# A two-layer encoder on one core: v, q's sums and the attention output turned in 32x32 blocks on VectorE instead of on TensorE

## The chip, the cores and the metric

The kernel runs on one core of one Trainium2 chip. The metric is device time in microseconds of one execution; runs of the kernel before gave 774.77, 776.28 and 776.96, with the median 776.28. Profiles come from one further execution, in which the hardware profiler recorded every instruction. Engines in the profile: PE is TensorE's matrix multiply, PEld its loading of weights, DVE is VectorE, ACT ScalarE, POOL GpSimd, and SP the engine that only issues DMAs here.

## What is computed

Two pre-norm residual layers over 256 tokens of 1024 channels, in float32, and a final RMSNorm. Each layer projects the normalised input once into eleven segments, and runs two token mixers beside each other, a gated delta rule in both directions and a differential softmax attention:

```python
h = rmsnorm(x, norm_w[l]); proj = h @ w_in[l]
# delta branch: 8 heads of 128, chunks; q, k, v pass a 5-tap convolution and SiLU
qkv = silu(short_conv(concatenate([q, k, v]), conv_w))
q, k = l2norm(heads(q)), l2norm(heads(k))            # per token and head
o = rmsnorm(o_fwd + o_bwd, norm_w)                    # delta rule forward and backward
y_a = o * silu(z_a)
# attention branch: 8 heads, two softmaxes of 64 channels each
a = softmax(q0 k0) - lam * softmax(q1 k1)
y_b = rmsnorm(a @ v, subln_w) * (1 - lambda_init) * silu(z_b)
x = x + (sigmoid(gate_a) * (y_a @ w_pa) + sigmoid(gate_b) * (y_b @ w_pb)) @ w_out
```

## The kernel before

**Projections.** Tokens lie in two tiles of 128 (`NM` is 2). Every float32 product is made of three matmuls in the rounded format fp32r: each weight tile and each activation is split into a rounded part `hi` and the rest `lo`, and hi·hi, lo·hi and hi·lo are summed in PSUM (lines 244 to 246, 282, and 298 to 302). `weights` (L207) loads a pair of 128-row weight tiles over SP's queue into `raw`, which ScalarE rounds into `hi` (L230) and VectorE subtracts to `lo` (L232). Three raw, two hi and two lo buffers let this run two pairs ahead of TensorE. A projection of 512 columns is 48 matmuls. In `proj_tm` (L237) and `proj_by_tile` (L259) tokens are the output rows; in `proj_fm` (L287) channels are.

**Turning.** A 128x128 transpose is a matmul against `ident` into PSUM. `split_T` (L184) turns four of them and writes hi and lo from there. It serves h, the two gated outputs yb and ya, and the merged output. In `conv` (L517), channels are rows while the taps run along tokens (L524, L528) and SiLU follows (L532, L537); then each pair of channel tiles is turned (L545). For k the turned tile is copied (L552) and its squares summed per token by ScalarE (L557); for q only the squares are summed, into `ssq`; for v the turned tile is scaled by `nrm`, k's factor, on VectorE (L548).

**The delta chain.** k's sums and the gates give log decays (`log_decays`, L567). `decays` (L618) loads them broadcast from DRAM, 512 KB for four heads and one token tile, over POOL's queue (L622), masks them with affine_select (L628) and has ScalarE take the exponentials, 32 per layer (L632). `weigh_k` and `weigh_q` multiply products k·k and k·q by them (L639, L643). `turn_blocks` (L654) moves 32x32 diagonal blocks through DRAM, `substitute` (L670) inverts them on VectorE in 31 steps, `spread_blocks` (L677) writes the result to DRAM (`udr`), and `merges` (L701) reads it back (L709, L713) and joins blocks to 64 and 128. `chunks` (L779) then runs the states: y1, sp, ks, y2, qs, po, each four matmuls per group of four heads, copied out of PSUM by ScalarE or VectorE before the next. Its output lands in q's place in `kq` (L818, L828).

**Attention.** `head` (L834) makes two score products on two row halves of TensorE (L844), maxima on VectorE (L851), exponentials on ScalarE (L853), the difference on VectorE (L861), four turns (L864), the product with v (L870) and its sum of squares (L876).

**Order.** A scheduler orders each engine's instructions by priority, which follows the program's order unless `tc.high_priority` raises it, and by when its own time model has them ready. `behind(ins)` queues an instruction behind `ins` where both are on the same engine; it adds no wait. `mark` keeps the instructions that these refer to; `mark["done", kt]` is the last matmul of step kt of the latest `proj_tm`. Per layer the program has: v of attention, k (two convolutions), log decays, q (two), decays and k·k, q and k of attention, substitution, v (two), then heads 0 to 7 among the projections zb and za, merges and chunks at high priority, the gating of yb (`gated`, L955), the projections gb, pb, ga, the gating of ya, pa, the merged output and o. The long projections fill TensorE while the chains wait for other engines.

**Rings.** `work` and `wpool` hand out buffers by tag: `w2c` has three of 2 KB per partition, shared by small tiles of several stages; `vf` two.

The functions that the diff touches, and what calls them, with the profile's line numbers:

## Time and profile before

| | |
|---|---|
| median of three runs | 776.28 us (774.77 to 776.96) |
| the profiled execution | 779.15 us |
| its span, first to last instruction | 777.3 us |
| mean granted TensorE clock | 0.995 |
| PEld busy | 649.4 us, 84% |
| a turn of 128x128 on TensorE, record | 270 to 273 ns |
| HBM | 121.27 MB read, 4.75 MB written |

A busy share is the share of the span in which an engine ran at least one instruction. Records of matmuls overlap, because they are pipelined: what one costs is the distance from its start to the next start, and not its duration. In a group's line, the numbers behind the shapes are the count, the busy time in us, the mean ns of one, and the idle time of the engine ahead of them with what ended it. In a waits line they are the total, the times and the longest. The chain of waits follows the execution back from its last instruction, from each step to what released it. Layer 0 takes about the first half of the span and layer 1 the second; the two look alike.

### The profile page before, as it was taken

To read this page: it belongs to the slowest core of one execution; us is meant where nothing else is said; L and a number is where in the kernel's file an instruction comes from. 1 tells how busy PE (TensorE), PEld (TensorE's weight loads), DVE (VectorE), ACT (ScalarE), POOL (GpSimd) and SP (SyncE) were. 2 spreads that over 40 slices of the span, in tenths; PEclk is the share of its full clock that TensorE was granted. 3 is DMA by queue.
4 is the path that set the end of the run, shared out by engine and by line. 5 is a ranking of instruction groups with operands and counts; after the bars stand their busy time and mean duration, and the time that the engine had idled before them with its cause. 6 is when DMAs were issued, how large, how long until landed. Compare 5 with 4: busy or idle time off the path is not lost.

```text
span 777.3 us, 13803 instructions
## 1 busy us (share of the span) xinstructions
PE 758.6 (98%) x5222; PEld 649.4 (84%) x5222; DVE 562.4 (72%) x1057; ACT 470.8 (61%) x1036; POOL 98.8 (13%) x137
## 2 busy tenths in 40 slices
PE   7999999999999999999999998999999999999996
PEld 4899889977878888877889888989788788888784
DVE  5686889999974635377677777999998653536782
ACT  5647776556767744564455668565677676356551
POOL 5100422100320000010010034210005010001000
PEclk9999999999999999999999999999999999999998
DMA  7762767654594544346675255766557754343631
GB/s 226 220 195 61 216 191 205 179 172 126 153 204 147 193 135 136 109 156 206 207 224 140 78 165 217 200 181 175 142 147 179 186 163 161 114 133 112 213 110 54
DMA packets 77745, 126.91 MB, mean 163 GB/s; under 512 B 19679, under 2 KB 20015, under 8 KB 77680
## 3 DMA queue, kind: packets, MB, share of 16 engines
q1 hardware_dynamic: 71038, 112.99, 49.5%
q0 software_dynamic: 3936, 9.77, 4.6%
q10 hardware_dynamic: 2706, 3.28, 1.3%
q8 instruction: 41, 0.67, 0.4%
q14 instruction: 24, 0.20, 0.1%
HBM read 121.27 MB, written 4.75 MB: 162 GB/s over the span
## 4 chain that ended last, share of the span: by engine, by line
PE 79%; DVE 10%; DMA 5%; ACT 3%; issue 2%; POOL 0%; SPq 0%; POOLq 0%; DVEq 0%; ACTq 0%
PE pp_vb L282 5%; PE pp_qk L244 2%; PE sc L844 2%; PE pp_qk L245 2%; PE pp_o L282 2%; DMA raw_vb<-in_w_in_dram 2%; PE pp_qk L246 2%; PE av L870 2%; PE pp_za L245 2%; PE pp_gb L245 2%; PE pp_gb L244 2%; PE pp_za L246 2%; PE pp_pb L246 2%; PE pp_pb L245 2%; PE pp_ga L246 2%
## 5 line engine op out<-in xcount | busy, mean ns | idle before, releaser
L245 PE MATMUL pp_qk<-lo_qk,hT 128*128 128x512 f32 x128 | 50.6, 395 | 0.0
L246 PE MATMUL pp_qk<-hi_qk,hT 128*128 128x512 f32 x128 | 50.0, 390 | 0.0
L244 PE MATMUL pp_qk<-hi_qk,hT 128*128 128x512 f32 x128 | 45.5, 396 | 0.0
L232 DVE TENSOR_TENSOR lo_pb<-raw_pb,hi_pb 128x1024 fp32r<-128x1024 f32 x16 | 19.6, 1224 | 35.7 <-ACT hi_pb L230 35.7
L230 ACT CAST hi_qk<-raw_qk 128x1024 fp32r<-128x1024 f32 x28 | 29.4, 1051 | 26.1 <-PE pp_qk L246 15.5
L232 DVE TENSOR_TENSOR lo_qk<-raw_qk,hi_qk 128x1024 fp32r<-128x1024 f32 x32 | 39.1, 1221 | 6.0 <-ACT hi_qk L230 5.7
L298 PE MATMUL pf_q<-hT,hi_q 128*128 128x256 f32 x128 | 37.0, 292 | 1.8 <-DVE hi_q L230 1.8
L853 ACT ACTIVATE es<-sc,mx 128x256 f32<-128x256 f32 x64 | 29.8, 474 | 13.0 <-DVE mx L851 13.0
L302 PE MATMUL pf_q<-hT,lo_q 128*128 128x256 f32 x128 | 36.6, 299 | 0.7 <-DVE lo_q L232 0.6
L300 PE MATMUL pf_q<-hT,hi_q 128*128 128x256 f32 x128 | 36.5, 288 | 0.0
L298 PE MATMUL pf_v<-hT,hi_v 128*128 128x256 f32 x128 | 36.2, 287 | 0.0
L300 PE MATMUL pf_v<-hT,hi_v 128*128 128x256 f32 x128 | 35.9, 284 | 0.0
L298 PE MATMUL pf_k<-hT,hi_k 128*128 128x256 f32 x128 | 35.8, 285 | 0.0
L300 PE MATMUL pf_k<-hT,hi_k 128*128 128x256 f32 x128 | 35.6, 283 | 0.0
L232 DVE TENSOR_TENSOR lo_gb<-raw_gb,hi_gb 128x1024 fp32r<-128x1024 f32 x16 | 19.6, 1224 | 21.5 <-ACT hi_gb L230 21.3
L232 DVE TENSOR_TENSOR lo_ga<-raw_ga,hi_ga 128x1024 fp32r<-128x1024 f32 x16 | 19.6, 1225 | 21.0 <-ACT hi_ga L230 21.0
L302 PE MATMUL pf_k<-hT,lo_k 128*128 128x256 f32 x128 | 34.4, 284 | 0.4 <-DVE lo_k L232 0.4
L302 PE MATMUL pf_v<-hT,lo_v 128*128 128x256 f32 x128 | 34.5, 288 | 0.0
L230 ACT CAST hi_pb<-raw_pb 128x1024 fp32r<-128x1024 f32 x16 | 16.8, 1049 | 25.1 <-PE pp_pb L246 24.3
L528 DVE SCALAR_TENSOR_TENSOR cvq<-pf_q,cw,cvq 128x254 f32<-128x254 f32 (+1 forms) x64 | 29.5, 476 | 1.9 <-ACT cvq L524 1.4
L528 DVE SCALAR_TENSOR_TENSOR cvk<-pf_k,cw,cvk 128x254 f32<-128x254 f32 (+1 forms) x64 | 28.5, 478 | 2.0 <-ACT cvk L524 1.3
L528 DVE SCALAR_TENSOR_TENSOR cvv<-pf_v,cw,cvv 128x254 f32<-128x254 f32 (+1 forms) x64 | 29.8, 479 | 0.0
(358 smaller groups left out, 2496.9 us busy)
## 6 DMA issues: line engine op xcount, KB each, us to landing
raw_qk<-in_w_in_dram SPq DMA_DIRECT2D x32, 512.0 KB, 3.8
raw_k<-in_w_in_dram SPq DMA_DIRECT2D x16, 512.0 KB, 4.8
raw_q<-in_w_in_dram SPq DMA_DIRECT2D x16, 512.0 KB, 3.7
raw_v<-in_w_in_dram SPq DMA_DIRECT2D x16, 512.0 KB, 3.7
raw_zb<-in_w_in_dram SPq DMA_DIRECT2D x16, 512.0 KB, 3.7
raw_za<-in_w_in_dram SPq DMA_DIRECT2D x16, 512.0 KB, 4.5
raw_gb<-in_w_in_dram SPq DMA_DIRECT2D x16, 512.0 KB, 4.7
raw_o<-in_w_out_dram SPq DMA_DIRECT2D x16, 512.0 KB, 4.6
```

Source lines behind the costliest of these rows:

```text
L230: high = (V.tensor_copy if kp in turned else S.copy)(hi[:, :, :n], raw[:, :, :n]).ins
L232: mark[nm, kp] = high, V.tensor_tensor(lo[:, :, :n], raw[:, :, :n], hi[:, :, :n].bitcast(F32), ALU.subtract).ins
L244: T.matmul(o, act[kt // 4][:, 0, kt % 4, ts_], hi, start=kt == 0, stop=False)
L245: T.matmul(o, act[kt // 4][:, 0, kt % 4, ts_], lo, start=False, stop=False)
L246: mark["proj"] = T.matmul(o, act[kt // 4][:, 1, kt % 4, ts_], hi, start=False, stop=kt == KT - 1).ins
L282: mark["proj"] = T.matmul(o, a_, w_, start=kt == 0 and a_ is ah and w_ is hi, stop=kt == KT - 1 and a_ is al).ins
L298: T.matmul(o, hi[:, cs], act[kt // 4][:, 0, kt % 4, :], start=first, stop=False, skip_group_check=True)
L300: T.matmul(o, hi[:, cs], act[kt // 4][:, 1, kt % 4, :], start=False, stop=False, skip_group_check=True)
L302: T.matmul(o, lo[:, cs], act[kt // 4][:, 0, kt % 4, :], start=False, stop=done, skip_group_check=True)
L528: V.scalar_tensor_tensor(ca[:, o0:o1], acc[:, b, o0 + sft : o1 + sft], cw[:, j, cb : cb + 1], ca[:, o0:o1], ALU.mult, ALU.add)
L844: mm = T.matmul(sp[n][:, qt * SEQ : (qt + 1) * SEQ], qkT[h // 4][rows, 0, h % 4, qt * P : (qt + 1) * P], qkT[h // 4][rows, 1, h % 4, :], s ...
L853: S.activation(es[:, n, qt, :], spv[:, qt, :], AF.Exp, bias=mx[:, n, qt : qt + 1], accum_out=s_all[:, h, n, qt : qt + 1])
```

## The change

Three sets of turns leave TensorE. A block transpose on VectorE turns the sixteen 32x32 blocks of each 128x128 square in place, for four squares (512 columns) at once; a write of 256 KB to DRAM and four reads of 64 KB, all issued by POOL, then put the blocks where a full transpose would have them. This serves v (both tiles of a pair in one transpose, k's factor applied by ScalarE as it copies the landed blocks into `vtm`) and yb (`split_B` in place of `split_T`). For q's sums, `key_sums` transposes blocks, squares them on ScalarE, sums 32 at a time on VectorE, and passes only the partial sums through DRAM.

Beside that: the loads of the decays of heads 4 to 7 are queued behind POOL's last affine_select of heads 0 to 3's first tile (`cut`), where `seen` held ScalarE's exponentials; heads 1 to 5 get fixed places behind the middle or the end of a projection, with their four scores kept together; `weigh_q` and the first merge products move to the projection za 1; and pa's third weight pair gets a home in A's memory.

```diff
+    def squares(nm):
+        return work.tile([P, 4, 4, 32], F32, tag="tb", name=f"tb_{nm}", bufs=2)
+    def turn_squares(tb, src):
+        return V.transpose(tb, src.rearrange("p k (j t) -> p j k t", j=4)).ins
+    def bounce(tb, nm):
+        dd = dram.tile([4, 32, 4, P], F32, tag="bnc", name=f"bnc_{nm}", bufs=4)
+        G.dma_start(out=dd.rearrange("i t j x -> (i t) (j x)"), in_=tb.rearrange("p j k t -> p (j k t)"))
+        land = work.tile([P, 4, 4, 32], F32, tag="w2c", name=f"land_{nm}", bufs=3)
+        for j in range(4):
+            G.dma_start(out=land[blk(j)].rearrange("t i k d -> t i (k d)"),
+                        in_=dd[:, :, j].rearrange("i t x -> t i x"))
+        return land
+    def split_B(dst, src, m, nm, w):
+        tb = squares(f"{nm}{m}")
+        turn_squares(tb, src)
+        land = bounce(tb, f"{nm}{m}")
+        flat_ = squares(f"w{nm}{m}").rearrange("p a b t -> p a (b t)")
+        S.activation(flat_.rearrange("p k (i t) -> p k i t", i=4), land.rearrange("p i k t -> p k i t"),
+                     AF.Copy, scale=w)
...
+        S.copy(hi, flat_)
+        V.tensor_tensor(lo, flat_, hi.bitcast(F32), ALU.subtract)
...
+                if seg == "q":
+                    return
+                if seg == "v":
+                    tb = squares(f"v{l}{g}{b0}")
+                    turn_squares(tb, ths.rearrange("p b (m t) -> p (b m) t", m=NM))
+                    land = bounce(tb, f"v{l}{g}{b0}")
+                    for b in range(2):
+                        for m in range(NM):
+                            hd = 4 * g + b0 + b
+                            S.activation(vtm[:, m, hd, :].rearrange("p (i d) -> p i d", i=4),
+                                         land[:, :, 2 * b + m, :], AF.Copy, scale=nrm[:, m, hd : hd + 1])
+                    return
...
-                if seg == "v":
-                    V.tensor_tensor(vtm[:, :, bs, :].rearrange("p m b d -> p b m d"), ptv,
-                                    last(nrm[:, :, bs].rearrange("p m b -> p b m"), P), ALU.mult)
-                    return
...
+                mark["cut"] = G.affine_select(
...
-            first = mark["done", 5] if g == 0 else None
+            first = mark["done", 7] if g == 0 else None
...
+        def key_sums():
+            for h in range(0, NH, 2):
+                tb = squares(f"q{l}{h}")
+                with behind(mark["spread"]):
+                    turn_squares(tb, kq[:, h : h + 2, :, 1, :].rearrange("p h m t -> p (h m) t"))
+                S.activation(tb, tb, AF.Square)
+                V.tensor_reduce(qpart[:, :, h : h + 2, :].rearrange("p j h m -> p j (h m)"), tb,
+                                AX.X, ALU.add)
+            G.dma_start(out=qdr.rearrange("i t j x -> (i t) (j x)"),
+                        in_=qpart.rearrange("p j h m -> p (j h m)"))
+            for j in range(4):
+                G.dma_start(out=qsum[blk(j)], in_=qdr[:, :, j].rearrange("i t x -> t i x"))
+            V.tensor_reduce(ssq.rearrange("p m h -> p h m"),
+                            qsum.rearrange("p i (h m) -> p h m i", m=NM), AX.X, ALU.add)
...
-                for n in (1, 0):
+                for n in (1, 0) if after is None else (0, 1):
...
-                    with nullcontext() if n else tc.high_priority(offset=HP):
+                    with behind(None if qt or n or after is None else mark["done", after]), \
+                            tc.high_priority(offset=HP) if qt or not n or after is not None else nullcontext():
...
-        seen = mark["decay", 0], mark["decay", 1]
+        cut = mark["cut"]
...
-        decays(1, 0, seen[0])
+        decays(1, 0, cut)
...
-        decays(1, 1, seen[1])
+        decays(1, 1, cut)
...
-        head(1)
+        head(1, 7)
...
-        head(2)
-        head(3)
+        head(2, 3)
+        head(3, 7)
...
-        head(4)
-        head(5)
+        head(4, 3)
+        head(5, 7)
+        z_part(za, C_ZA, "za", 1)
         for g in range(2):
             for c in range(NM):
-                weigh_q(g, c, mark["done", 4 * g + 2 * c + 1])
-        z_part(za, C_ZA, "za", 1)
+                weigh_q(g, c, mark["done", 2 * g + c])
+        key_sums()
...
+        gated(lambda i, m: heads4(ob[i][:, m, :]), zb, rb, nw[:, 1:2], ybT, f"yb{l}",
+              split=split_B)
...
-        branch(yaT, w_pa[l], gta, f"pa{l}")
+        branch(yaT, w_pa[l], gta, f"pa{l}", [None, None, *homes((("A", 1),), f"pa{l}"), None])
...
-                later={2: mark[f"pa{l}0", 1], 3: mark[f"pa{l}0", 3]})
+                later={2: mark[f"pa{l}0", 2], 3: mark[f"pa{l}0", 3]})
```

More of the change, by code (lines that the diff above doesn't have):

```diff
@@ L833, in hybrid_encoder, with head @@
         ob = e4(f"ob{l}", "eo")
-        def head(h):
+        def head(h, after=None):
             es = work.tile([P, 2, NM, SEQ], F32, tag="w4a", name=f"es{l}{h}", bufs=2)
@@ L846, in head @@
                                       qkT[h // 4][rows, 1, h % 4, :], start=True, stop=True)
-                    if qt or not n:
+                    if qt or n != (after is None):
                         tc.keep_in_program_order(mm)
```

36 lines of the change are left out of this document (20 added, 16 removed).

## The prediction

> **What bounds the kernel now.** I read the page's engine line first, then the table by windows for three stretches that the change touches, then the waits of TensorE.
>
> ```profile
> PE 758.6 (98%) x5222; PEld 649.4 (84%) x5222; DVE 562.4 (72%) x1057; ACT 470.8 (61%) x1036; POOL 98.8 (13%) x137
> ```
> ```profile
> 104.00:206.00 102.00, 101.84 (x597) 87.02 (x598) 98.65 (x218) 65.07 (x148) 7.77 (x9) 1.00 0.59 167
> 206.00:232.00 26.00, 26.00 (x157) 21.07 (x156) 21.88 (x31) 17.13 (x49) 11.51 (x16) 1.00 0.88 186
> ...
> 257.00:278.00 21.00, 21.00 (x201) 18.57 (x197) 12.46 (x23) 14.84 (x25) 0.00 (x0) 1.00 0.54 185
> ```
> ```profile
> PE pf_q L298 <- DVE hi_q L230: 1.8, 1, 1.8
> ...
> PE pp_pa L245 <- DVE lo_pa L232: 1.1, 2, 0.5
> ...
> PE pf_q L302 <- DVE lo_q L232: 0.6, 1, 0.6
> ...
> PE ctq L545 <- DVE kq L537: 0.3, 1, 0.3
> ```
>
> TensorE is the bound. A window's columns are PE, PEld, DVE, ACT, POOL, the clock, the DMA share and GB/s, and PE fills all three but for 0.16 us. Work taken off it is time saved as long as the other engines keep up; from 104 to 206 VectorE, at 98.65 of 102 us, could hardly do more. TensorE's own waits are few, and the largest are for q's weights.
>
> **Turns taken off TensorE.** Per layer 16 turns of q, 16 of v and 16 of the gated output go, 96 in all, mostly in pairs:
>
> ```profile
> 140.41 0.39 PE L246 MATMUL pp_qk<-hi_qk,hT 128*128 128x512 f32 x1
> 140.64 0.38 PE L545 MATMUL ctv<-ident,thv 128*128 128x128 f32 x2
> 140.78 0.71 PE L244 MATMUL pp_qk<-hi_qk,hT 128*128 128x512 f32 x2
> 141.32 0.40 PE L245 MATMUL pp_qk<-lo_qk,hT 128*128 128x512 f32 x1
> ```
>
> Durations overlap, so I count starts. A matmul holds the next back by 0.23 (140.41 to 140.64). The pair moves the next one from 140.64 to 140.78, and the two behind it take 0.54 instead of 0.46: 0.14 + 0.08 = 0.22 us. 48 pairs by 0.22 are 10.6 us, 3.5 each for q, v and the gated output.
>
> **The decay loads move.** `seen` names ACT's exponentials, but the loads stand in POOL's queue, and the trace shows all four leaving together. `cut` is POOL's own affine_select, so two of the four now leave behind it, at about 96.9 instead of 89:
>
> ```profile
> 88.07 2.18 POOL L622 DMA_DIRECT2D B<-gdr  x4 [1.83 <-ACT E L599]
> ...
> 95.66 1.22 POOL L628 TENSOR_SCALAR_AFFINE_SELECT B<-B 128x512 f32<-128x512 f32 x2
> ```
> ```profile
> raw_q<-in_w_in_dram SPq DMA_DIRECT2D x16, 512.0 KB, 3.7
> ```
> ```profile
> 465.65 12.34 DMA raw_q<-in_w_in_dram
> ```
> ```profile
> 470.00:480.00 10.00, 8.18 (x67) 7.95 (x64) 4.55 (x8) 9.22 (x31) 6.08 (x11) 0.96 0.73 283
> 480.00:490.00 10.00, 9.85 (x59) 8.85 (x58) 9.86 (x15) 5.74 (x21) 1.89 (x2) 0.87 0.46 118
> ```
>
> A load of q's weights, 3.7 us in the median, took 12.34 beside these 2 MB. Beside 1 MB I expect about half the excess gone, 4 us, and then the q waits, 1.8 + 0.6 + 0.3 = 2.7 us, go. Behind the longest of them the granted clock fell to 0.96 and 0.87 in two windows of 10 us, 0.4 + 1.3 = 1.7 us, which goes too: 4.4. If the loads gain nothing, the term is nothing. What comes late instead is the decays of the second four heads, and with them the start of the substitution, by up to 2 us. The Trainium skill (TensorE: Matmul & The Clock Gate, Part 1) lets the clock drop only after an idle window of about 3.4 us. The trace disagrees: here 1.8 us was enough. By the page the term would be 2.7.
>
> **Heads.** Head 1's scores are cut in two, head 2's are whole:
>
> ```profile
> 176.73 0.62 PE sc L844 x2
> ...
> 183.93 1.06 PE sc L844 x6
> ...
> 191.78 1.06 PE sc L844 x8
> ```
>
> 0.62 + 1.06 against 1.06: kept together, head 1 saves 0.6 per layer, 1.2. The other marks put heads where the trace already has them, about one per half projection; I cost them at nothing, under the projection between.
>
> **branch pa.** Its third weight pair gets a home in A, free since the last po, and needn't wait for a slot. The waits for lo_pa, 1.1, go.
>
> **What the other engines get.** The trace has no block transpose. The nearest rows:
>
> ```profile
> L548 DVE TENSOR_TENSOR vtm<-ctv,nrm 128x512 f32<-128x512 f32 x8 | 5.5, 686 | 0.0
> L851 DVE TENSOR_REDUCE mx<-sc 128x2 f32<-128x512 f32 x32 | 21.1, 685 | 1.2 <-PE sc L844 1.2
> L866 ACT COPY aT<-at 128x512 f32<-128x512 f32 x16 | 9.3, 580 | 5.7 <-PE at L864 5.7
> L557 ACT ACTIVATE sqj<-ctq 128x128 f32<-128x128 f32 x32 | 8.8, 274 | 1.2 <-PE ctq L545 0.7
> L557 ACT ACTIVATION_READ_ACCUMULATOR sqj<-ctq 128x1 f32 x32 | 6.3, 197 | 0.0
> ```
> ```profile
> 104.34 0.68 DVE L230 CAST hi_qk<-raw_qk 128x1024 fp32r<-128x1024 f32 x1
> ...
> 129.45 1.14 DVE L668 COPY la<-lt 64x1024 f32<-64x1024 f32 x1
> ```
>
> A transpose of 512 columns lies between 0.34 (half the plain cast of 1024) and 1.14 (the strided copy of 1024). I take 0.69, as the other passes over 512 columns. Then v costs VectorE nothing, four transposes for four products (by the ends, 1.4 us less to 1.8 more per layer). q's four transposes and four reductions, 5.5 us, come behind the substitution (`spread`), where the second window has 4.1 us free. The gated output's four transposes, 2.8, fall into the third window, where VectorE has 8.5 of 21 us free and POOL all.
>
> ScalarE loses 16 squares with their reads (7.5 us a layer) and gains 16 copies of v (4.4), four squares of q (2.3) and four more passes of the gated output (2.3): +1.5, where a third of it is free. The eight bounces of v and the gated output move 0.5 MB each, q's far less; I cost the bandwidth at nothing, since the DMA share is 0.59. With q's they are 45 issues a layer on POOL.
>
> **New waits.** ScalarE's v copies wait for landings; queued behind them are the hi casts of qk, v and zb, for which VectorE's lo and then TensorE wait. Two weight pairs lie ready, 24 matmuls of 0.23 or 5.5 us, and cover a late landing, so I take nothing; without cover each of the eight bounces costs some 2 us. q's last reduction waits on VectorE in the same way, with lo splits behind it. q's five issues share POOL's queue with the merge loads, 3.3 us if they come ahead of them.
>
> **The merge chain.**
>
> ```profile
> L727 PE MATMUL y64p<-T,A x128: 184/191/212, 232.7 to 237.5; 32*32 32x32 f32 x128
> ...
> L709 SPq DMA_DIRECT2D T<-udr x4: 482/940/1141, 219.8 to 222.7; - x4
> ...
> DMA to landing us min/median/max: 3.8/4.8/5.5
> ```
> ```profile
> 339.77 2.18 DVE L960 SCALAR_TENSOR_TENSOR kq<-kq,ro,za 128x128 f32<-128x128 f32 x8
> ```
> ```profile
> 342.09 0.39 PE L246 MATMUL pp_ga<-hi_ga,hT 128*128 128x512 f32 x1
> 342.32 0.38 PE L189 MATMUL pt_ya<-ident,kq 128*128 128x128 f32 x2
> ```
>
> The merges' last input lands by 222.7 + 5.5 = 228.2, and they start at 232.7: 4.5 us of room to come earlier. From there the chain runs over copies and additions to the delta gating, which ends at 341.95, just when ga, the last filler, ends. So what is saved ahead of the merges counts; what is saved behind them, the gated output's 3.5 us (1.75 per layer), leaves TensorE idle before pt_ya. I count it as nothing. Of the two idle times I charge one with a clock drop as above, 1.7.
>
> **The gated output's bounce.**
>
> ```profile
> 255.40 4.29 DVE L960 SCALAR_TENSOR_TENSOR ob<-ob,rb,zb 128x128 f32<-128x128 f32 x16
> ```
> ```profile
> L244 PE MATMUL pp_pb<-hi_pb,ybT x64: 387/389/476, 277.8 to 688.2; 128*128 128x512 f32 x64
> ```
> ```profile
> 285.20 0.62 PE L244 MATMUL pp_pb<-hi_pb,ybT 128*128 128x512 f32 x2
> ```
> ```profile
> udr<-X POOLq DMA_DIRECT2D x4, 256.0 KB, 4.4
> ...
> T<-udr POOLq DMA_DIRECT2D x8, 64.0 KB, 5.1
> ```
> ```profile
> L709 POOL DMA_DIRECT2D T<-udr x8 | 5.2, 664 | 4.2 <-DMA udr<-lt 4.2
> ```
>
> A tile needs its products (1.1) and transpose (0.7), the write (4.4), four issues (2.7), a landing (5.1), two ScalarE passes and a subtraction (1.9): the first is ready at 255.4 + 15.9 = 271.3. With writes overlapping reads, POOL's five issues (3.3) set the pace and the fourth comes at 281.2. pb wants the first two at 277.8 and the last two at 285.2. The heads before it and pb itself move up together, so I compare in the times of before: just in time, hidden by gb and pb's first half. If that cover is gone, each us of lateness is one of TensorE.
>
> **Sum.** On the profiled execution (span 777.3, 779.15 with what lies around it): q 3.5 + v 3.5 + loads 4.4 + head 1.2 + pa 1.1 = 13.7, less 1.7: 12.0, so 767.1. The median of the runs is 2.9 below that execution: 776.3 - 12.0 = 764.3.
>
> **Rivals.**
> - All of the gated output's turns count too: 12.0 + 3.5 + 1.7 = 17.2, 759.1. It needs a chain with slack; ga's end at 342.3 against 341.95 speaks against it.
> - VectorE sets the merges. It is full to 206, and a late substitution (2 us) leaves 2.5 of the 4.5 us of room: 2 x 2.5 + 1.1 - 1.7 = 4.4, 771.9; with transposes at 1.14 another 2 x 1.8 goes, 775.5. For it speaks a rule of the Trainium skill (VectorE: DVE Perf Modes, Rules for kernel authors): turn 128x128 on TensorE where PSUM will do as destination, as it did here.
> - Slower: the gated output comes late. If POOL's queue holds each tile's reads ahead of the next write, a tile takes 0.7 + 4.4 + 2.7 = 7.8 us, and the fourth is ready at 271.3 + 3 x 7.8 = 294.7, 9.5 us after 285.2. TensorE waits in pb, the chain's matmuls queued behind it, and both layers drop the clock: 764.3 + 2 x 9.5 + 1.7 = 785.0. It decides from a fourth tile later than 285.2. For it: one queue, two buffers of the tile; against: POOL has nothing else to do in the third window.
> - Slower as well: v's landings uncovered, 8 x 2 = 16 us: 780.
> - The decay loads don't help: 4.4 less, 768.7.
>
> **Chances.** Forecast 0.42, loads without help 0.10, all counts 0.10, VectorE 0.17, late output 0.13, landings 0.08. The likeliest one's own range is 759 to 770; the whole, 757 to 781, leaves out the late output and a little beyond either end. A measurement tells 0.3% (2.3 us) from no change: below 774.0 lie the first three and most of VectorE's, 0.72; within, 0.07; slower 0.21.
>
> **What would show it.** Right: no ctq, ctv, pt_yb rows; B loads in two bursts and no PE wait for hi_q; whole heads; transposes near 0.69; y64p some 4 to 6 us earlier; no PE wait for ybT; a short one at pt_ya. Wrong: TensorE waiting for ybT or for hi casts behind v copies, the substitution's end not earlier, or a clock below 0.95 in new windows.

## The result, and the profile after

The changed kernel takes 804.35 us (median of four runs, 800.35 to 807.44) against 775.69 before: a ratio of 1.0365, 95% interval 1.0316 to 1.0414. It is slower by 28 us, where 12 us less was forecast. The span of the profiled execution grew by 21.1 us, from 777.3 to 798.4, and its mean clock fell from 0.995 to 0.985. The traces show less of it than the medians: the execution profiled before took 779.15, above its kernel's median, and the one profiled now, 800.35, is the shortest of its four.

The engine line of the page, and TensorE's waits (total, times, longest, in us):

```profile
PE 755.8 (95%) x5126; PEld 644.4 (81%) x5126; DVE 582.8 (73%) x1083; ACT 479.3 (60%) x1020; POOL 148.8 (19%) x227
```
```profile
PE sc L905 <- ACT stg L474: 6.4, 4, 3.0
PE pp_za L277 <- DVE lo_za L264: 5.4, 3, 3.7
PE pp_pa L276 <- ACT hi_pa L262: 3.8, 2, 2.1
...
PE qs L828 <- ACT kq L858: 2.3, 2, 1.2
PE at L925 <- issue: 2.3, 1, 2.3
PE pp_pa L277 <- DVE lo_pa L264: 1.8, 2, 0.9
PE pp_za L276 <- DVE za L344: 1.6, 1, 1.6
...
PE pp_pb L276 <- ACT ybT L230: 1.2, 2, 0.6
```

The 96 turns are gone (5222 records before, 5126 now), but TensorE is busy only 2.8 us less: part of what the turns saved is eaten by matmuls at half clock. By the mean clocks, what is lost to it grew from 0.005 x 777.3 = 3.9 to 0.015 x 798.4 = 12.0 us. Idle time grew from 777.3 - 758.6 = 18.7 to 798.4 - 755.8 = 42.6 us. So the growth of the span, 23.9 - 2.8 = 21.1 us, is new waiting and the clock behind it. None of the eight waits listed stood among those of before, but for 1.1 of the 1.8 us for `lo_pa`. The waits for q's weights are gone. The table by windows says where (TensorE, PEld, VectorE, ScalarE, POOL, clock, DMA share, GB/s):

```profile
104.00:206.00 102.00, 97.12 (x547) 81.35 (x547) 95.75 (x214) 65.42 (x141) 16.00 (x29) 0.98 0.63 183
206.00:232.00 26.00, 22.28 (x119) 17.64 (x119) 22.58 (x30) 16.73 (x41) 13.07 (x21) 0.93 0.83 173
257.00:278.00 21.00, 21.00 (x222) 18.12 (x221) 13.61 (x27) 13.99 (x22) 5.84 (x10) 1.00 0.74 239
160.00:170.00 10.00, 6.79 (x23) 4.60 (x23) 9.13 (x24) 5.66 (x16) 0.00 (x0) 0.83 0.56 160
210.00:220.00 10.00, 7.11 (x28) 5.99 (x29) 9.38 (x12) 4.55 (x14) 6.71 (x12) 0.83 0.70 189
550.00:560.00 10.00, 7.46 (x20) 5.06 (x21) 8.48 (x26) 6.30 (x18) 0.56 (x1) 0.66 0.37 107
```

The first two stretches were full in the kernel before; now TensorE lacks 4.9 and 3.7 us in them, at a lower clock. The operations that the change added cost about what the prediction took, except the copies of v (records of 0.39 us, 0.32 by busy time, for 0.274). Groups, with mean ns behind the bar:

```profile
L583 ACT ACTIVATE vtm<-land_v,nrm 128x128 f32<-128x128 f32 x32 | 10.2, 390 | 7.8 <-DMA land_v<-bnc_v 7.8
...
L133 DVE STREAM_TRANSPOSE tb_yb<-ob 128x512 f32<-128x512 f32 x8 | 5.7, 707 | 1.6 <-DMA bnc_yb<-tb_yb 1.6
L133 DVE STREAM_TRANSPOSE tb_v<-thv 128x512 f32<-128x512 f32 x8 | 5.7, 707 | 0.0
...
L133 DVE STREAM_TRANSPOSE tb_q<-kq 128x512 f32<-128x512 f32 x8 | 5.2, 680 | 0.0
```

So the added operations by themselves don't explain the time. The waits point at four places where something stands ahead of what TensorE needs: the score tiles, za's weights, pa's weights and the chain beside yb. The experiments take them one by one.

### The profile page after: what moved, and what is told of

It is laid out like the page before. It is cut to its first block, busy times and chain, and to the rows that moved or that the text cites. A ratio compares the mean times of both kernels' runs of the same rounds, so it can differ in the third digit from the quotient of the medians.

```text
span 798.4 us, 13800 instructions
## 1 busy us (share of the span) xinstructions
PE 755.8 (95%) x5126; PEld 644.4 (81%) x5126; DVE 582.8 (73%) x1083; ACT 479.3 (60%) x1020; POOL 148.8 (19%) x227
## 5 line engine op out<-in xcount | busy, mean ns | idle before, releaser
L334 PE MATMUL pf_q<-hT,lo_q 128*128 128x256 f32 x128 | 34.9, 285 | 0.0
L277 PE MATMUL pp_za<-lo_za,hT 128*128 128x512 f32 x64 | 26.3, 410 | 5.4 <-DVE lo_za L264 5.4
L277 PEld LDWEIGHTS pp_qk<-lo_qk,hT 128*128 128x128 f32 x128 | 24.0, 188 | 6.8 <-DVE lo_qk L264 2.0
```

Of the source, the lines that this page charges most:

```text
L277: T.matmul(o, act[kt // 4][:, 0, kt % 4, ts_], lo, start=False, stop=False)
L334: T.matmul(o, lo[:, cs], act[kt // 4][:, 0, kt % 4, :], start=False, stop=done, skip_group_check=True)
```

## The experiments

All medians are in us. A ratio is to the kernel before on the same chip, with its 95% interval. Below, gains and losses are differences of ratios, turned into us by 775.5, and the waits are those of one profiled execution each. In the text under an expectation, "the rival" is the second of the outcomes that it names.

| run | what it is | median | ratio |
|---|---|---|---|
| no_v | changed, v as before | 788.92 | 1.0169 (1.0140 to 1.0198) |
| no_q | changed, q's sums as before | 792.28 | 1.0237 (1.0201 to 1.0273) |
| no_yb | changed, yb as before | 799.58 | 1.0320 (1.0303 to 1.0337) |
| no_pa | changed, pa as before | 797.35 | 1.0299 (1.0252 to 1.0346) |
| no_vqpa | changed, v, q and pa as before | 792.38 | 1.0223 (1.0204 to 1.0242) |
| v_late | changed, v's copies later | 798.39 | 1.0292 (1.0274 to 1.0311) |
| ktm_V | changed, POOL's products on VectorE | 793.45 | 1.0247 (1.0202 to 1.0292) |
| old_order | changed, order of before | 797.21 | 1.0261 (1.0236 to 1.0286) |
| only_cut | before, decay loads moved | 770.98 | 0.9943 (0.9927 to 0.9960) |
| ord_cut | only_cut and the new order | 784.65 | 1.0110 (1.0089 to 1.0132) |
| cut_heads | only_cut and the heads' places | 775.59 | 1.0002 (0.9988 to 1.0015) |
| cut_q | only_cut and q's sums | 781.42 | 1.0071 (1.0043 to 1.0099) |
| cut_qlate | the same, later | 774.86 | 0.9991 (0.9980 to 1.0001) |
| cut_v | only_cut and v | 771.02 | 0.9937 (0.9912 to 0.9962) |
| cut_yb | only_cut and yb | 777.99 | 1.0018 (0.9994 to 1.0042) |
| cut_yb1 | the same, another ring | 766.29 | 0.9880 (0.9858 to 0.9903) |
| mend_q | cut_yb1, q late, products moved | 771.88 | 0.9950 (0.9935 to 0.9965) |
| mend_vq | mend_q and v | 783.76 | 1.0101 (1.0070 to 1.0132) |

### The decay loads alone

```diff
-        seen = mark["decay", 0], mark["decay", 1]
+        cut = mark["cut"]
...
-        decays(1, 0, seen[0])
+        decays(1, 0, cut)
```

> The kernel before with the decay loads of heads 4 to 7 behind POOL's affine_select and nothing else. The prediction's term: the waits for q's weights (2.7 us) and the clock drop behind them (1.7 us) go, 4.4 us, 771.9 us. Rival (a load spread out costs elsewhere, the decays and the substitution start later): 776 us, with waits at the merges or at the decay products.

The ratio falls by 0.0057, 4.4 us: the size that was forecast. POOL's rows of the first layer, and the window of the second in which the clock had dropped to 0.87:

```profile
86.97 1.14 POOL L655 DMA_DIRECT2D B<-gdr  x2 [1.83 <-ACT E L632]
...
93.74 1.10 POOL L655 DMA_DIRECT2D B<-gdr  x2
```
```profile
480.00:490.00 10.00, 10.00 (x54) 8.57 (x53) 9.69 (x18) 4.74 (x11) 2.45 (x4) 1.00 0.56 166
```

The loads leave in two bursts, TensorE has no wait for q's weights left, and the clock stays at 1.00. That the size fits is partly chance. Of the 4.4 us, 1.7 were the half clock behind the wait, which the profiled execution of before had (mean clock 0.995); the seven executions of before that this run is compared with had 0.997 or 0.998, so little of it was in them to gain. And the kernel differs from before in two more small parts of the change: `th` of a pair of channel tiles lies in one buffer, so that the ring `vf` is twice as large, and one weight load of the first layer is marked later (`k{l}1`, 0 to 1). No run separates them from the loads. For the loads speaks the place: in the traces the stretch of q's matmuls is some 1.5 us shorter in the first layer and 3.9 in the second, while those of v agree within 0.1. This kernel is the base of the runs whose names begin with cut.

### Undoing one part at a time

```diff
-                if seg == "v":
-                    tb = squares(f"v{l}{g}{b0}")
...
+                if seg == "v":
+                    V.tensor_tensor(vtm[:, :, bs, :].rearrange("p m b d -> p b m d"), ptv,
```

> The changed kernel with v as before: 16 turns a layer on TensorE and the product with k's factor on VectorE; all else as changed. Theory A (ScalarE's copies of v wait in its queue for POOL's landings, with the copies of the score tiles behind them, so TensorE waits 3.0 us a layer for sc and the clock drops behind it, 1.7 and 3.4 us): the two waits of sc for ACT L474 go, the granted clock stays above 0.95 there, 11 us are gained and 3.5 us for the turns given back: 0.99 of the changed kernel, about 797 us. Rival (the new order of heads and products makes those waits): sc still waits for about 3 us, and the time is 804 + 3.5 = 808 us.

15.2 us less: twice what was expected. No wait of sc for stg is left. The rows of ScalarE in the changed kernel show why it was there:

```profile
162.48 1.28 ACT L583 ACTIVATE vtm<-land_v,nrm 128x128 f32<-128x128 f32 x4 [1.89 <-DMA land_v<-bnc_v]
163.67 0.56 ACT L474 COPY stg<-pp_qk 128x512 f32<-128x512 f32 x1
...
165.08 0.58 ACT L474 COPY stg<-pp_qk 128x512 f32<-128x512 f32 x1
```

ScalarE waits 1.89 us for a landing, then makes four copies of v, and only then copies the tiles (L474) out of PSUM from which `sc` is to be made. TensorE waits 2.5 us here and 3.0 in the second layer, and a stretch of half clock (3.4 and 6.8 us) follows each.

```diff
-        key_sums()
...
+                ss = ssk if seg == "k" else ssq
```

> The changed kernel with q's sums as before: 16 turns a layer on TensorE and squares on ScalarE, no block transposes behind the substitution. Theory B (VectorE's q transposes stand between the substitution's end and the lo splits of za, so that POOL's four products of ktm take the memory port first and the lo_za subtraction lasts 4.7 us instead of 1.2): lo_za's rows return to 1.2 to 1.5 us, the waits of pp_za for lo_za (5.4 us in all) and the clock drop at 210 to 220 go, about 8 us, and 3.5 us for the turns are given back: about 800 us. Rival (POOL's products and VectorE meet there whatever q does, by the new order): a row of about 4 us stays, and the time is 804 + 3.5 = 808 us.

9.9 us less, twice what theory B expected, and no row of lo_za above 2.07 us. The wait of sc for stg is gone here too, though v is as changed. What makes the lo_za rows long is settled only below.

```diff
-              split=split_B)
+        gated(lambda i, m: heads4(ob[i][:, m, :]), zb, rb, nw[:, 1:2], ybT, f"yb{l}")
```

> The changed kernel with the attention output yb turned on TensorE as before. Theory C (the bounce of yb is late or blocks ScalarE ahead of the chain's copies): the waits for ybT (1.2 + 0.8) and of qs for kq (2.3) go, and the chain is not longer: at most 4 to 5 us gained against 3.5 us given back for the turns, so 802 to 805 us. Rival (the bounce is covered, and the turns count in full because the chain is ready early, as pt_ya at 326 shows): 804 + 3.5 = 808 us.

3.5 us less, with intervals that overlap, so yb loses or gains little net in this surrounding. The waits for ybT and kq are gone, as theory C has it, but those for lo_za grow from 5.4 to 8.1 us.

```diff
-        branch(yaT, w_pa[l], gta, f"pa{l}", [None, None, *homes((("A", 1),), f"pa{l}"), None])
+        branch(yaT, w_pa[l], gta, f"pa{l}")
...
-                later={2: mark[f"pa{l}0", 2], 3: mark[f"pa{l}0", 3]})
+                later={2: mark[f"pa{l}0", 1], 3: mark[f"pa{l}0", 3]})
```

> The changed kernel without the home for pa's third weight pair in A. Theory D (the home puts the cast of the third pair ahead of that of the second in ScalarE's queue, so hi_pa comes late: 2.1 + 1.8 us of waits and a half clock at 740 to 750, 1.6 us): the waits of pp_pa for hi_pa go, only about 1.1 us for lo_pa as in the kernel before stay, and the time is about 799 us. Rival (pa's waits come from ga ending at a different time against the weights, or from the delta gating): waits of 2 to 4 us stay at pa and the time is within 2 us of 804 us.

7 us less by the medians, 5.1 by the ratios (their intervals overlap), and all waits in pa are gone, even those for `lo_pa`: theory D. ScalarE's rows of the changed kernel:

```profile
351.59 1.05 ACT L262 CAST wA_pa<-raw_pa 128x1024 fp32r<-128x1024 f32 x1 [1.47 <-DMA raw_pa<-in_w_pa_dram]
352.55 1.04 ACT L262 CAST wktm_o<-raw_o 128x1024 fp32r<-128x1024 f32 x1
353.49 1.04 ACT L262 CAST hi_pa<-raw_pa 128x1024 fp32r<-128x1024 f32 x1
```

The cast into A (the third pair) waits for its load, and with a cast for o stands ahead of the pair that TensorE needs next.

```diff
-                    land = bounce(tb, f"v{l}{g}{b0}")
...
-        key_sums()
...
+        branch(yaT, w_pa[l], gta, f"pa{l}")
```

> The changed kernel with v, q's sums and pa as before: what is left of the change is the decay loads, the new order of heads and products, and yb's bounce. If the three undoings alone (15.4, 12.1 and 7.0 us) act in separate places, they add: 804.4 - 34.5 = 770 us, and no wait of TensorE of over 1 us for lo_za, stg or hi_pa is left. Rival (they remove one another's stalls, since each moves the same queues): the sum is less, 780 to 790 us, and a wait for another operand stands in the same stretch.

The rival holds: at 1.0223 the three undoings gain 11.0 us together, less than v's alone. In this kernel TensorE waits 6.4 us for lo_za again, though q's transposes are gone. Theory B as I had put it falls: the transposes are not needed for the long row.

### What makes the lo_za rows long

```diff
-                with behind(mark["udr"]):
-                    G.tensor_tensor(st[d], st[d], last(kds[:, d, hs4], P), ALU.mult)
+                with behind(mark["spread"]):
+                    V.tensor_tensor(st[d], st[d], last(kds[:, d, hs4], P), ALU.mult)
```

> The changed kernel with the four products of ktm by the decays on VectorE, behind the substitution's last copy, in place of POOL. Theory B (POOL's four products, 1.03 us each, keep VectorE out of memory for 3.5 us): the lo_za row of 4.7 us is gone and all lo_za rows lie near 1.2 us; VectorE pays about 4 x 0.7 = 2.8 us, so the waits of pp_za shrink by 3 to 5 us, and with less of a clock drop the time is about 796 us. The udr writes of lt, which stand behind the products in POOL's queue, leave about 4 us earlier. Rival (the row is long because of the block transposes or of DMA descriptors): it stays long without POOL's products.

9.2 us less, and no lo_za row in that stretch above 1.24 us. TensorE's waits for lo_za shrink from 5.4 to 2.5 us; new are 4.2 us for A. VectorE's rows in the kernel before, then in the changed one, each with POOL's:

```profile
207.78 1.23 DVE L232 TENSOR_TENSOR lo_za<-raw_za,hi_za 128x1024 fp32r<-128x1024 f32 x1
...
209.53 1.45 DVE L232 TENSOR_TENSOR lo_za<-raw_za,hi_za 128x1024 fp32r<-128x1024 f32 x1
```
```profile
208.57 5.31 POOL L800 TENSOR_TENSOR ktm<-ktm,kds 128x512 f32<-128x512 f32 x4
```
```profile
206.94 1.28 DVE L133 STREAM_TRANSPOSE tb_q<-kq 128x512 f32<-128x512 f32 x2
208.16 5.82 DVE L264 TENSOR_TENSOR lo_za<-raw_za,hi_za 128x1024 fp32r<-128x1024 f32 x2
```
```profile
207.72 4.03 POOL L840 TENSOR_TENSOR ktm<-ktm,kds 128x512 f32<-128x512 f32 x4
```

Before, VectorE's subtraction was running when POOL started, and the two took turns: POOL's products take 5.31 us instead of 4.03. In the changed kernel VectorE is at a block transpose when POOL starts, and the subtraction that follows waits until all four products are done: the two subtractions take 5.82 us, with 3.4 us of standing. VectorE's subtraction and POOL's products shut each other out. The Trainium skill (SBUF — State Buffer, "SBUF: two separate sides") says that the port pair that both use is an exclusive lock, held for a whole instruction. The trace agrees that one is shut out, but it is shut out for four instructions in a row, not for one.

Which of the two happens can be read from the 17 traces in which POOL makes these products. In five of them, in both layers, a subtraction of VectorE had started 0.62 to 0.81 us before the first product and was still running; there the two take turns. In the other twelve, VectorE's subtraction (in no_v the copy of `lt`, in cut_v's second layer a product for `cc`) started at most 0.55 us before the first product, or behind it, and stood until the fourth was done. To start first is thus not enough. In most of them POOL starts some 0.7 us behind the end of VectorE's copy of `lt`, so what differs is whether a subtraction follows that copy at once (before, only_cut) or something else does: a transpose, a maximum, or a short wait. This is a pattern of the rows; no run moved that start alone, and the reason stays open.

```diff
-        head(1, 7)
+        head(1)
...
-                weigh_q(g, c, mark["done", 2 * g + c])
+                weigh_q(g, c, mark["done", 4 * g + 2 * c + 1])
...
-            first = mark["done", 7] if g == 0 else None
+            first = mark["done", 5] if g == 0 else None
```

> The changed kernel with the order of before for heads, weigh_q and merges; v, q's sums and yb are turned on VectorE, the loads and pa are as changed. Theory E (the order costs some 15 to 20 us): about 787 us, without the 3.7 us wait for lo_za in both layers. Rival (the new order is there because the blocks need it; the stalls come from v's landings and from q's transposes): 800 us or more, with sc waiting for stg still.

The ratio is 1.0261, 8.1 us less. The rival is right that sc still waits for stg (6.5 us): that wait is not the new order's. And lo_za lasts 4.71 us here too, so the old order doesn't keep it away by itself.

### The new order alone

Of the change, `cut` and these parts:

```diff
+        head(1, 7)
...
+                weigh_q(g, c, mark["done", 2 * g + c])
...
+            first = mark["done", 7] if g == 0 else None
```

> The kernel before with the decay loads moved and the new order (heads 1 to 5 behind fixed matmuls, weigh_q and the first merge products in za 1) and nothing else: no turn leaves TensorE. Theory E (the new order itself costs: it puts the merges' products later and lets a head run where VectorE is late): since the changed kernel without v, q's sums and pa's home still took 792.4 us, and the loads alone 771.0, the order holds most of these 21 us: 785 to 790 us, with the long lo_za rows opposite POOL's products and a wait at the merges (z). Rival (the prediction: the marks put heads where the trace had them, at no cost, and head 1 gains 1.2 us): 770 us; the 21 us are then yb's bounce.

Theory E holds: 0.0167, 13.0 us lost without one turn moved. TensorE waits 3.2 us for lo_za in each layer, and in the first also 2.4 us in the merges (z), for which the profile shows no releaser.

Of these, the heads' places alone:

```diff
-        head(2)
-        head(3)
+        head(2, 3)
+        head(3, 7)
```

> The kernel before with the decay loads moved and the new places of heads 1 to 5, but the products of weigh_q and merges in their old places. Theory G (the heads' places cost nothing and the late products and merges hold the 13.7 us of the new order): 770 us (771.0 less 1.2 for head 1 kept whole). Rival (heads put behind fixed matmuls crowd VectorE and shift the substitution's end so that POOL's products take the port): 776 us or more, with the lo_za rows of over 4 us.

The rival holds: 0.0059, 4.6 us lost. The rows at the end of the substitution, VectorE's and POOL's:

```profile
203.70 6.67 DVE L264 TENSOR_TENSOR lo_za<-raw_za,hi_za 128x1024 fp32r<-128x1024 f32 x2 [0.29 <-ACT hi_za L262]
```
```profile
204.11 4.03 POOL L834 TENSOR_TENSOR ktm<-ktm,kds 128x512 f32<-128x512 f32 x4
```

Again POOL's products, at full pace, shut out two subtractions (6.67 us for 2.4), and TensorE waits 1.9 us a layer for them. In only_cut the first subtraction starts at 204.86, right behind the copy of `lt` and 0.79 us before POOL; here it waits 0.29 us for its cast and starts only 0.41 us before POOL, although both come over a microsecond earlier. By difference, the other 8.4 us of the order are those of the later products.

### q's sums and v alone

Of the change, `cut` and `key_sums`, in the order of before:

```diff
+                if seg == "q":
+                    return
...
+        key_sums()
```

> The kernel before with the decay loads moved and q's sums by block transposes (key_sums), in the order of before. If q's part is sound by itself, 16 turns a layer go at no new wait: 771.0 - 3.5 = 767.5 us. Rival (the transposes and sums behind the substitution put VectorE's lo splits of za behind them, or let POOL's products take the port first): a wait for lo_za of 3 us or more a layer, 775 us or more.

The rival holds in time, though not in the size of its waits: 9.9 us lost; lo_za rows of 4.72 and 4.71 us, waits of 1.6 and 1.3 us behind them, and 1.0 us more for za in each layer.

```diff
-                with behind(mark["spread"]):
+                with behind(mark["silu"]):
                     turn_squares(tb, kq[:, h : h + 2, :, 1, :].rearrange("p h m t -> p (h m) t"))
...
+          with behind(mark["evp"]):
             V.tensor_reduce(ssq.rearrange("p m h -> p h m"),
```

> The kernel before with the decay loads moved and q's sums by block transposes, but these queued on VectorE behind the last SiLU of za (about 230 us) in place of behind the substitution, and their last sum behind pb's last evacuation. Theory H (VectorE is the limit from about 100 to 220 us, and what is added behind the substitution delays za's lo splits and the merges' products): the 10.4 us of loss go, and some of the 2.7 us of turns are gained: 768 to 771 us. Rival (the turns taken from q's convolution or the missing squares shift the order in some other way): 775 us or more.

By 0.0080, 6.2 us of the 9.9 are back, not all: lo_za still lasts 5.3 us in each layer, though no transpose of q stands there any more. VectorE's maximum takes the place behind the copy of `lt`.

Of the change, `cut` and v's bounce:

```diff
+                    land = bounce(tb, f"v{l}{g}{b0}")
...
-                    V.tensor_tensor(vtm[:, :, bs, :].rearrange("p m b d -> p b m d"), ptv,
```

> The kernel before with the decay loads moved and v turned in blocks on VectorE through DRAM, in the order of before. Theory A (ScalarE's copies wait for landings ahead of the copies of the score tiles): sc or hi casts wait 2 to 3 us a layer and a clock drop follows: 771.0 - 3.5 + 11 = 778 us. Rival (prediction: the landings are covered): 767.5 us.

Neither holds: 0.5 us gained, within the interval. By distances of starts the 16 turns of v had cost 1.34 us a layer. In the first layer zb's 49th matmul starts at 181.24 instead of 183.11, but the first of gb at 238.06 and 238.12: between the two, where one lo_za row lasts 5.30 us, the gain is gone. TensorE's idle time there is only 0.4 us, so the rest of it stays open. In the second layer TensorE waits 1.4 us for `es` ahead of gb, with a stretch of half clock behind it. ScalarE's rows:

```profile
162.99 0.59 ACT L474 COPY stg<-pp_qk 128x512 f32<-128x512 f32 x1 [0.98 <-PE pp_qk L278]
...
164.62 0.58 ACT L474 COPY stg<-pp_qk 128x512 f32<-128x512 f32 x1
166.09 1.28 ACT L581 ACTIVATE vtm<-land_v,nrm 128x128 f32<-128x128 f32 x4 [0.89 <-DMA land_v<-bnc_v]
```

Here the scheduler put the copies of v behind the score tiles' copies, and nobody waits. With q's turns gone as well it puts them ahead: sc waits for stg in all seven traces that have v and q both off TensorE, and in neither of the two with v alone (no_q, cut_v).

```diff
+                    mark["stg"] = S.copy(st, ps).ins
...
+                        with behind(mark["stg"]):
+                            S.activation(vtm[:, m, hd, :].rearrange("p (i d) -> p i d", i=4),
...
         head(0)
+        v_copies()
```

> The changed kernel, with ScalarE's copies of landed v queued behind the copies of the last q and k tiles of the attention (stg) and written later in the program; transposes, bounces and landings stay. Theory A (only the place of the waiting copies in ScalarE's queue costs): TensorE's waits of sc for stg (6.4 us) go with the clock drops behind them (5 us), and the time is near 789 us, as with v undone altogether, or below, since the turns stay off TensorE. Rival (VectorE's transposes of v, or POOL's queue with eight bounces, are what costs): sc still waits, or another wait of that size comes instead, and the time stays above 799 us.

5.7 us less than changed, not 15: sc's wait falls from 6.4 to 1.9 us, so the place in ScalarE's queue was the cause of it. But waits of zb for its weights and for cvv come instead (2.4 + 2.1 + 1.7 us), those of pb for ybT grow from 1.2 to 3.4, and the long lo_za rows stay.

### yb's ring

Of the change, `cut` and yb's bounce, then the same with another ring:

```diff
+              split=split_B)
```

> The kernel before with the decay loads moved and yb's bounce, in the order of before. Theory F (each tile takes two of the ring's two buffers, one to transpose and one to scale, so the third transpose waits until the first tile is split; tiles come some 9 us apart, the fourth about 30 us behind the first, and pb and the chain behind it wait): the loss seen with the new order, 7 to 8 us, is here too: about 778 us, with the transposes of yb 6 to 11 us apart. Rival (the loss came from the new order's later merges beside it): 768 to 771 us.

Theory F holds by its size: 0.0075, 5.8 us lost. POOL's rows of the first layer, writes (L138) and reads (L141) of the four tiles:

```profile
258.53 0.66 POOL L138 DMA_DIRECT2D bnc_yb<-tb_yb  x1 [7.33 <-DVE tb_yb L133]
264.32 2.19 POOL L141 DMA_DIRECT2D land_yb<-bnc_yb  x4 [5.13 <-DMA bnc_yb<-tb_yb]
266.50 0.56 POOL L138 DMA_DIRECT2D bnc_yb<-tb_yb  x1
270.65 2.18 POOL L141 DMA_DIRECT2D land_yb<-bnc_yb  x4 [3.58 <-ACT tb_wyb L226]
275.50 0.56 POOL L138 DMA_DIRECT2D bnc_yb<-tb_yb  x1 [2.67 <-DVE tb_yb L133]
...
287.45 0.56 POOL L138 DMA_DIRECT2D bnc_yb<-tb_yb  x1 [5.70 <-DVE tb_yb L133]
292.71 2.18 POOL L141 DMA_DIRECT2D land_yb<-bnc_yb  x4 [4.70 <-ACT kq L852]
```

The fourth tile is written 28.9 us behind the first. The ring `tb` has two buffers, and a tile needs two: one to transpose, one to scale. That is theory F, and the writes come 8 to 12 us apart. But the longest wait of TensorE (3.8 us for A, and a half clock) lies in the second layer, and isn't shown to be the ring's: there the first write takes 9.0 us to its reads, beside a stream of weight loads, and ScalarE waits for that landing ahead of a copy of the chain:

```profile
649.71 0.72 ACT L226 ACTIVATE tb_wyb<-land_yb,nw 128x512 f32<-128x512 f32 x1 [5.98 <-DMA land_yb<-bnc_yb]
650.33 0.57 ACT L830 COPY A<-y1p 128x512 f32<-128x512 f32 x1
```

```diff
-        flat_ = squares(f"w{nm}{m}").rearrange("p a b t -> p a (b t)")
+        flat_ = work.tile([P, 4, P], F32, tag="w2a", name=f"w{nm}{m}", bufs=2)
```

> The same as the run with yb alone, but the scaled copy of each tile lies in the ring of the score tiles (two buffers, free at that time), so that the ring of two serves the transposes alone. Theory F: the four transposes come at most 5 us apart, the fourth tile is ready 10 us or more earlier, the waits in pb go: 768 to 771 us, since 16 turns a layer (1.5 us) are off TensorE. Rival (POOL's queue, in which each tile's reads wait for its write and stand ahead of the next write, sets the pace): transposes stay 7 us apart or more, and the time is that of the run with yb alone, about 778 us.

0.9880, the fastest of all kernels, 9.3 us under before:

```profile
257.94 1.22 POOL L138 DMA_DIRECT2D bnc_yb<-tb_yb  x2 [7.34 <-DVE tb_yb L133]
264.19 4.38 POOL L141 DMA_DIRECT2D land_yb<-bnc_yb  x8 [5.03 <-PE y1p L822]
268.56 1.11 POOL L138 DMA_DIRECT2D bnc_yb<-tb_yb  x2
275.67 4.37 POOL L141 DMA_DIRECT2D land_yb<-bnc_yb  x8 [6.00 <-PE sp L822]
```

Two tiles go together, and the second pair is written 10.6 us behind the first; in the second layer the first write takes 6.6 us to its reads. The ratio is 0.0063, 4.9 us, under that of only_cut: the 16 turns a layer, 1.54 us by distances of starts, explain 3.1, and the waits of pa for lo_pa that are gone another 1.1. From gb's first matmul to the first turn of the merged output, the first layer takes 115.8 us, with the narrow ring 117.7, and 117.4 in only_cut. So the ring is shown for 1.9 us in the first layer, without the slow write. In the second layer the same stretch takes 115.5 and 123.4 us; of these 7.9 us, 3.8 are the wait for A and some 1.7 the half clock behind it, and whether the ring leads to the slow write stays open. It may not come each time: the ten executions of cut_yb lie between 770.60 and 779.76.

### All mended

cut_yb1, key_sums behind head 7, and POOL's products there too, on VectorE:

```diff
-                with behind(mark["udr"]):
-                    G.tensor_tensor(st[d], st[d], last(kds[:, d, hs4], P), ALU.mult)
+                with behind(mark["es"]):
+                    V.tensor_tensor(st[d], st[d], last(kds[:, d, hs4], P), ALU.mult)
```

> The kernel before with the decay loads moved, yb in blocks with its scaled copies in a ring of their own (766.3 us so far), q's sums in blocks queued behind head 7 with their bounce behind yb's on POOL, and the four products of ktm on VectorE behind head 7 in place of POOL. If the place and POOL's products were the cause: every lo_za row near 1.2 us, no clock drop near 210, and the 16 turns of q (1.3 us a layer) count: 763 to 764 us. Rival (VectorE's extra 8 us a layer behind head 7 delay lo_gb or yb): waits of pp_gb for lo_gb or of pp_pb for ybT of 2 us or more, 767 us or more.

The rival holds in another form: 5.4 us more than cut_yb1. All lo_za rows at the end of the substitution are 1.22 or 1.23 us, so nothing holds them up. But in the second layer yb's first transpose starts at 636.63, in cut_yb1 at 629.50, 7.1 us behind, where gb's first matmul was 3.6 us behind. ScalarE's first pass of yb there waits 4.91 us for its landing, with the copies of y1p behind it: TensorE waits 2.6 us for A, and elsewhere 1.4 for ktm and 1.4 for es. q's sums gained in none of the three places where they were put (in the third they moved together with POOL's products).

And v's bounce:

```diff
+                    land = bounce(tb, f"v{l}{g}{b0}")
```

> The same with v turned in blocks through DRAM as in the changed kernel, so that all three sets of turns are off TensorE as the change meant. v alone gave 771.0 against 771.0, its 1.3 us a layer lost to VectorE before za. With VectorE free of the products at the end of the substitution: 761 to 763 us. Rival (ScalarE's v copies meet the score tiles, as in the changed kernel, since q's turns no longer hold TensorE back): sc waits for stg 2 to 3 us a layer with a clock drop, 768 to 775 us.

The rival holds, and by more than it said: 11.7 us more than mend_q. sc waits 6.0 us for stg, and a pass of yb, which waits 5.42 us for its landing, holds the chain for 3.2. v's copies:

```profile
164.21 1.28 ACT L583 ACTIVATE vtm<-land_v,nrm 128x128 f32<-128x128 f32 x4 [1.78 <-DMA land_v<-bnc_v]
165.40 0.56 ACT L474 COPY stg<-pp_qk 128x512 f32<-128x512 f32 x1
```

The same order as in the changed kernel, in the old order of heads, with POOL's products away: v together with q is enough.

## Why the prediction was wrong, point by point

The steps that failed are those that put at nothing what the moved work meets in the order of the other engines. In the sum, q stood for 3.5 us gained, and its run lost 9.9; v for 3.5, gained 0.5 by itself; the heads for 1.2, and the new order lost 13.0; pa for 1.1, lost 5.1; yb for nothing, lost 5.8. Only the loads came out.

- **The bound.** TensorE is the bound over the whole, but up to 232 the turns of q and v were worth little or less than nothing. I had read that VectorE "could hardly do more" and still counted 7.0 us for them. v gave 0.5 us by itself, and q's lost 9.9. The rival on VectorE had the right place, though not what happens there.
- **Turns.** 1.34 us (v) and 1.54 (yb) per layer by distances, 2.7 and 3.1 in two layers, for 3.5: a little too high.
- **Decay loads.** 4.4 us forecast, 4.4 measured. The waits went as forecast; that the size fits is partly chance, since the half clock that makes 1.7 of it shows in none of the seven executions of before that the run is compared with.
- **Heads.** "I cost them at nothing", and 1.2 us for head 1 kept whole: this step failed. The heads' places lose 4.6 us, and the order as a whole 13.0. I looked for the heads' own cost on TensorE, and not at what a shift of VectorE's queue by tenths of a microsecond would meet: POOL's products.
- **pa.** 1.1 us gained: failed, 5.1 lost. Its cast is queued on ScalarE ahead of another that is due sooner.
- **New waits.** "I take nothing": failed. I had named the hi casts behind v's copies; what stood behind them were the copies of the score tiles, which no weight pair covers. The rival "landings uncovered" (16 us) had the size, v's undoing gave 15.2 us, but by luck: it counted 2 us at each of eight bounces, and TensorE's waits are 6.4 us in two places with half clock behind them. It needs q's turns gone too.
- **yb's bounce.** The fourth tile "comes at 281.2", just in time: failed. The late-output rival named the two buffers of the tile and a queue, and took 7.8 us a tile; the writes of cut_yb come 8 to 12 apart in the first layer, and the fourth tile of the changed kernel is split at 303.34. That each tile takes two buffers I hadn't counted.
- **The merge chain.** "I count it as nothing", for the chain would end as ga ends: failed in the other direction. The delta output is turned at 326.45 and 333.25, with 70 matmuls of ga behind the second:

```profile
326.45 1.03 PE L208 MATMUL pt_ya<-ident,kq 128*128 128x128 f32 x8
...
333.25 1.03 PE L208 MATMUL pt_ya<-ident,kq 128*128 128x128 f32 x8
```

  The chain has slack, so yb's turns count. In cut_yb1, where ga isn't late, the second is at 333.50 and ga's last matmul at 339.15; in only_cut, with yb's turns on TensorE, they are at 338.94 and 338.71.
- **Not in it at all:** that POOL and VectorE shut each other out. Of the 17 traces in which POOL makes these products, 12 have a VectorE row of 4.1 to 5.5 us beside them, and TensorE waits up to 4.4 us a layer for it; five have them by turns: the kernel before, only_cut, cut_yb, cut_yb1 and no_q.

The parts add up only roughly. On only_cut: order 13.0, q 9.9, yb 5.8 (8.8 with the new order), v -0.5; pa 5.1 in the changed kernel; less 4.4 for the loads: about 29 to 32, against 28.3. That is partly chance, since the undoings don't add: v's stall needs q's turns gone, and several parts lead to the same shut-out. What stays open: why POOL's four products come by turns with VectorE's subtraction when that is well under way, and in one go otherwise.

## What to carry to other kernels

Before work is moved to an engine with a queue in fixed order, look for every instruction that will wait there for a landing, and for what stands behind it: here one copy that waits cost TensorE some 3 us and its clock. Count a ring's buffers per item, not per kind of use. A change of several parts is best measured part by part: two of these parts (the loads with what came along, and yb with one ring changed) give 9.3 us, and the others took back more than that.

## What the runs showed of the hardware

- After an idle time of TensorE of more than 2.2 us ahead of one instruction, the granted clock over the next 3 us was below 0.9 in 29 of 31 cases of these traces, often 0.50; after 1.3 to 2.2 us in 11 of 34. (The wait at the start of each trace, 3.1 us ahead of the first instruction, is left out.) The Trainium skill (TensorE: Matmul & The Clock Gate, Part 1) has about 3.4 us; the traces have less. Of 44 stretches of half clock in these traces, 26 lasted 3.41 us and 18 lasted 6.83; those at the very end of a trace are left out. An idle wait of 3 us with the shorter stretch behind it thus costs an estimated 4.7.
- A block transpose of 128x512 on VectorE takes 0.68 to 0.71 us and isn't held up beside POOL's products (206.94 and 1.28 for two, above, and 0.67 for one that lies wholly beside them in the second layer), while a subtraction of two SBUF operands is (4.1 to 5.5 us for 1.22).
- A bounce of 256 KB through DRAM takes POOL 0.6 us to issue the write and 2.2 for four reads; from the write's issue to the first read pass 4.1 to 9.0 us in the rows of cut_yb.
